# A chunked state-space stage: injection reordered on TensorE and ScalarE, products moved to GpSimd, tables and products of VectorE placed in PSUM

## Chip, cores and metric

The kernel runs on one core of one Trainium2 chip. The metric is device time in microseconds (us), the median of several executions of the whole program. Engines are named as in the profile: PE (TensorE, with PEld for its weight loads), DVE (VectorE), ACT (ScalarE), POOL (GpSimd) and SP (SyncE, which here only issues DMAs).

## What is computed

A two-layer network over 256 tokens of width 2048, in fp32: an S5 state-space mixer with a GLU, a feed-forward layer, shared keys and values with a dilated window attention, and a second feed-forward layer. The change lies in the S5 mixer alone. It has 128 groups of 16 channels, each with 64 complex states:

```python
lb = exp(lam * dt)                              # complex: lb_re, lb_im
bb = (lb - 1) / lam * B                         # input matrix, complex
bu = einsum('blgh,gph->blgp', u, bb)
s[l] = lb * s[l-1] + bu[l]                      # scan over the 256 tokens
y = Re(einsum('blgp,ghp->blgh', s, C)) + d_skip * u
g = gelu(y);  val, gate = split(g @ w_glu);  x = x + val * sigmoid(gate)
```

## The kernel before

The tokens are cut into 64 chunks of four. `s5_glu` does the whole stage; after it, dense blocks of products with weights split into a high and a low part run on PE to the end of the kernel.

The 128 groups are handled in four quarters (`qr` 0 to 3); a half (`h` 0 or 1) is two quarters and has its own state tile `sts[h]`. The parts, in the order in which the code issues them:

- **Tables.** DVE computes `lam` from the inputs, then its second, third and fourth powers (`power`, each kept as a 2x2 real form `pf[k]` by `form`), `gain` (B times a gain, into the last tap of `gps[qr]`), and `coefs` (15 small operations for the factor `cf`). ACT sums squares of the input; POOL raises the mean to -1/2 into `rc`; `scale_x` applies it on ACT.
- **`build_u(h)`**: PE transposes the input, ACT copies it under two masks into `ub[h]`.
- **`taps(qr)`**: for each of three taps and each of two components, a `pair`: one product of 512 columns and one sum of 256 columns on DVE.
- **`taps_inject(qr)`**, four rounds each: four transposes on PE into a `tr` tile, a copy on ACT to `gt`, sixteen products on PE into an `mm` tile, two copies on ACT into `sts`. All rounds stand in this order on PE and on ACT.
- **`build_c`**, **`powers(qr)`**: C times the factor, and C times the four powers (`fds[qr]`), as `pair`s on DVE.
- **`build_m(qr)`**: PE makes the in-chunk matrix of a quarter; `store_m(qr)` adds the skip term `dsm` on DVE and moves shifted rows with six DMAs on SP's queue.
- **`y_local`**: PE products of the in-chunk part.
- **`scan(nm, h)`**: 63 steps for each half, three DVE operations a step (a product of 128 columns with the fourth power's form, two sums of 64); `run` issues the two halves in turn, so six operations make a common step. "Chain a" is half 0, "chain b" half 1.
- **`y_state`** (PE, needs the finished states and `fds`), **`gelu`** (ACT), **`y_T`** (PE transposes, ACT high part, DVE low part), then `products` with the weights that `prepare` loaded and split.

`T`, `A`, `G` and `W` are PE, ACT, POOL and DVE with the order of the code kept: an instruction issued through them never passes an earlier one on its engine.

```python
        T, A, G, W = (InOrder(tc, e) for e in (nc.tensor, nc.scalar, nc.gpsimd, nc.vector))
```

Nearly all of their instructions therefore have line L57 in the profile, that of the wrapper; tiles tell them apart (`act_raw` tiles are called `actr` there). PSUM has eight banks: four for tiles `mm`, two for `tr`, two for `ms`. SBUF pools: `early` is released before the weights are opened, `late` after the mixer, `xres` (tag `xr`) has two buffers.

Of the kernel before, what the change touches and what calls it, by code (L numbers as in the profile page):

```python
# [2 lines left out]

# [8 lines left out]
FP32 = mybir.dt.float32  # L12
# [3 lines left out]
ALU = mybir.AluOpType  # L16
# [3 lines left out]
P = 128  # L20
# [8 lines left out]
GI = 16  # L29
NS = 64  # L30
# [29 lines left out]
class Net:  # L60
# [141 lines left out]
    def s5_glu(self):  # L202
        tc, nc, io = self.tc, self.nc, self.io
        late = tc.alloc_tile_pool(name="s5late", bufs=1)
        early = tc.alloc_tile_pool(name="s5early", bufs=1, side="right")
# [6 lines left out]
        ds = late.tile([P, 2, 64], FP32, name="ds")  # L212
# [30 lines left out]
        def tt(out, i, j, o, eng=None):  # L243
            (eng or V).tensor_tensor(out=out, in0=i, in1=j, op=o)
# [19 lines left out]
        for st in sts:  # L264
            G.memset(st[:, 0], 0.0)
        dsm = late.tile([P, 64, GI], FP32, name="dsm")
        tt(ds[:, 0], ds[:, 0], ds[:, 1], ALU.mult, G)
        tt(dsm, ds[:, 0].unsqueeze(2).broadcast_to([P, 64, GI]),
           dmask.unsqueeze(1).broadcast_to([P, 64, GI]), ALU.mult, G)

        ssc = early.tile([P, 2, 4], FP32, name="ssc")
        for q in range(2):
            for s in range(4):
                junk = early.tile([P, 32, GI], FP32, name="xjunk", tag="gt", bufs=4)
# [64 lines left out]
        gps = [early.tile([P, 2, 16, 4, GI], FP32, name=f"gp{qr}") for qr in range(2)]  # L339
        gps += [self.xres.tile([P, 2, 16, 4, GI], FP32, name="gpx", tag="xr") for _ in range(2)]  # L340

        def gain(qr):
            mo = 16 * qr
# [21 lines left out]
        def pair(out, f, src):  # L365
            pr = early.tile([P, 2, 16, GI], FP32, name="gpr", bufs=2)
            yield lambda: tt(pr, f.unsqueeze(3).broadcast_to([P, 2, 16, GI]), src, ALU.mult, W)
            yield lambda: tt(out, pr[:, 0], pr[:, 1], ALU.add, W)
# [8 lines left out]
        def taps_inject(qr):  # L377
            g, st, mo = gps[qr], sts[qr // 2], 16 * (qr % 2)
            for j2 in range(4):
                gtt = early.tile([P, 2, 2, P], FP32, name="gt", tag="gt", bufs=4)  # L380
                ps = self.ps_tr.tile([P, 2, 2, P], FP32, name="tr")
                for j in range(2):
                    for ri in range(2):
                        T.transpose(out=ps[:, j, ri],
                                    in_=g[:, ri, 4 * j2 + 2 * j:4 * j2 + 2 * j + 2].rearrange("p x s i -> p (x s i)"),
                                    identity=self.ident)
                A.copy(out=gtt, in_=ps)
                ps = self.ps_mm.tile([P, 2, 2, 2, NS], FP32, name="mm")
                for j in range(2):
                    ju = (qr % 2) * 8 + 2 * j2 + j  # L390
                    for ri in range(2):
                        for y in range(2):
                            T.matmul(ps[64 * y:64 * y + 64, j, ri],
                                     lhsT=gtt[:, j, ri, 64 * y:64 * y + 64],
                                     rhs=ub[qr // 2][:, ju, y].rearrange("p x c -> p (x c)"),
                                     start=True, stop=True)
                for j in range(2):
                    m0 = mo + 4 * j2 + 2 * j
                    A.copy(out=st[:, 1:64, :, m0:m0 + 2].rearrange("p c r m -> p r m c"),
                           in_=ps[:, j, :, :, 0:63])  # L400
# [4 lines left out]
        def coefs():  # L405
# [16 lines left out]
            yield lambda: tt(cf[:, 0, 1], t1, den, ALU.mult, W)  # L422
            yield lambda: W.tensor_copy(out=cf[:, 1, 0], in_=cf[:, 0, 1])

        def build_c(qr):
            mo = 16 * qr
            for k in range(2):
                yield from pair(cp[:, k, mo:mo + 16], cf[:, k, :, mo:mo + 16], ct[:, :, mo:mo + 16])

        def m_operand(qr, j4):  # L430
            m0 = 16 * qr + 8 * j4
# [25 lines left out]
                    nc.sync.dma_start(out=mt[64 * xx:64 * xx + n, t, mo:mo + 16],  # L457
                                      in_=mt[64 * xx + 64 - n:64 * xx + 64, 3, mo:mo + 16])

        def scan(nm, h):  # L460
            st = sts[h]
            f = pf[3][:, :, :, 32 * h:32 * h + 32]
            pr = late.tile([P, 2, 2, 32], FP32, name="spr" + nm)
            sm = late.tile([P, 2, 32], FP32, name="ssm" + nm)

            def step(c):
# [5 lines left out]
            for c in range(63):  # L472
                yield from step(c)
# [12 lines left out]

        def powers(qr):
            mo = 16 * qr
            for t in range(4):
                for k in range(2):  # L490
                    yield from pair(fds[qr][:, t, k], pf[t][:, :, k, mo:mo + 16], cp[:, :, mo:mo + 16])

        def y_local(qr, pool, nm):
            pss = [pool.tile([P, 8, 4, GI], FP32, name=nm) for _ in range(2)]
# [62 lines left out]
        fds = {0: fd[:, 0], 1: fd[:, 1]}  # L557
        run(*[build_c(qr) for qr in range(2)])
        run(*[build_c(qr) for qr in range(2, 4)])
        ms = {}  # L560
        for qr in range(4):
            ms[qr] = build_m(qr)
            if qr > 1:
                fds[qr] = self.xres.tile([P, 4, 2, 16, GI], FP32, name="fdx", tag="xr")
            run(powers(qr))
            if qr:
                store_m(qr - 1, ms[qr - 1])
        store_m(3, ms[3])
# [12 lines left out]

        prepare(0)
        y_state(0, yl[0])
        gms = {0: gelu(yl[0])}
        y_state(1, yl[1])
        gtile = [self.act_tile(), None]
        lhs = [gtile[0][:, k] for k in range(8)]
        y_T(0, gms[0])
        gms[1] = gelu(yl[1])
        gb0 = self.open_block(KT)  # L590
        for c in range(4):
            if c + 1 < 4:
                prepare(c + 1)
            for w in ws.pop(c):
                self.products(gb0, w, lhs, T)
            if c < 2:
                yl[c + 2] = y_local(c + 2, self.ps_ms, "ms")
                y_state(c + 2, yl[c + 2])
                gms[c + 2] = gelu(yl[c + 2])
            if c == 1:  # L600
                gtile[1] = self.act_tile()
                lhs += [gtile[1][:, k] for k in range(8)]
            if c < 3:
                y_T(c + 1, gms[c + 1])
# [325 lines left out]
```

## Time and profile before

| | |
|---|---|
| median of 3 runs | 2525.39 us (2515.63 to 2526.24) |
| profiled execution | 2518.62 us, span 2516.4 us |
| PE busy | 2403.2 us (96%) |
| DVE busy | 1361.6 us (54%) |
| ACT busy | 1080.2 us (43%) |
| POOL busy | 41.8 us (2%) |

The span runs from the first to the last instruction. A row of a list of instructions in order of time has its start in us, its length in us, the engine, the line, the operation, the tile written and the tiles read, the count, and in brackets the idle time before it with what ended it. A row that ends in "| a, b | c" is a group: busy time in us, mean length of one in ns, idle time before them in us. "PEclk" is the clock that the throttle granted to PE, 1.00 being full speed.

### The profile page before, as it was taken

Reading aid. Unit: us, or ns where it says so; the run is one execution under the profiler, and the core shown is the slowest. Engines: PE = TensorE matmul, PEld = TensorE weight load, DVE = VectorE, ACT = ScalarE, POOL = GpSimd, SP = SyncE. Lnnn points to the kernel's source line nnn. Section 1 sums busy time; section 2 is a strip of 40 time slices with the busy share of each in tenths; the row PEclk is TensorE's granted clock in tenths of the full one; section 3 lists DMA queues with packets and bytes.
Section 4 is the critical chain, followed back from the end, with each engine's and each line's share of the span. In section 5 each row is a group of like instructions: output and inputs, shape, how many; then the busy total and the mean of one; then the engine's idle time right before and its main releaser. Section 6 shows DMA issues by size and latency. Waiting matters only on the chain.

```text
span 2516.4 us, 28535 instructions
## 1 busy us (share of the span) xinstructions
PE 2403.2 (96%) x11456; PEld 1945.1 (77%) x11456; DVE 1361.6 (54%) x2033; ACT 1080.2 (43%) x1359; POOL 41.8 (2%) x33
## 2 busy tenths in 40 slices
PE   5619999999999999999999999999999999999999
PEld 4508888888888888888888888878888888888887
DVE  9493554544544444455544677765545444444444
ACT  5304444444433444455444555544444443344433
POOL 1000000000000000000000100000000000000000
PEclk7559999999999999999999999999999999999999
DMA  2014555555555555555555444445555555555554
GB/s 81 23 40 134 185 184 184 184 184 184 184 184 186 185 186 181 186 181 193 176 192 184 158 160 151 151 144 174 184 184 184 184 184 186 188 187 179 187 195 148
DMA packets 63028, 423.51 MB, mean 168 GB/s; under 512 B 8112, under 2 KB 9520, under 8 KB 12336
## 3 DMA queue, kind: packets, MB, share of 16 engines
q1 hardware_dynamic: 61744, 419.60, 48.8%
q8 instruction: 89, 1.46, 0.2%
q10 hardware_dynamic: 1152, 2.10, 0.2%
q14 instruction: 43, 0.35, 0.0%
HBM read 418.79 MB, written 2.10 MB: 167 GB/s over the span
## 4 chain that ended last, share of the span: by engine, by line
PE 93%; DVE 3%; ACT 0%; issue 0%; POOL 0%; POOLq 0%
PE mm L120 29%; PE mm L122 29%; PE mm L121 29%; PE ms L57 2%; PE mm L57 1%; PE ms L770 1%; DVE actr L57 1%; PE tr L656 1%; PE tr L721 1%; DVE sprb L57 1%; DVE spra L57 1%; PE tr L770 0%; PE tr L183 0%; DVE gpr L57 0%; DVE ssmb L57 0%; DVE ssma L57 0%
## 5 line engine op out<-in xcount | busy, mean ns | idle before, releaser
L102 DVE TENSOR_TENSOR wlo<-raw,whi 128x1024 fp32r<-128x1024 f32 x776 | 948.8, 1224 | 1002.3 <-ACT whi L101 1000.9
L101 ACT CAST whi<-raw 128x1024 fp32r<-128x1024 f32 x776 | 813.5, 1048 | 1160.4 <-PE mm L122 1143.4
L120 PE MATMUL mm<-whi,actt 128*128 128x512 f32 x3104 | 1235.9, 398 | 1.4 <-ACT whi L101 1.4
L122 PE MATMUL mm<-whi,actt 128*128 128x512 f32 x3104 | 1229.7, 396 | 0.0
L121 PE MATMUL mm<-wlo,actt 128*128 128x512 f32 x3104 | 1229.5, 396 | 0.0
L122 PEld LDWEIGHTS mm<-whi,actt 128*128 128x128 f32 x3104 | 583.2, 188 | 139.4
L120 PEld LDWEIGHTS mm<-whi,actt 128*128 128x128 f32 x3104 | 583.2, 188 | 138.6 <-ACT whi L101 2.1
L121 PEld LDWEIGHTS mm<-wlo,actt 128*128 128x128 f32 x3104 | 583.3, 188 | 137.1 <-DVE wlo L102 0.4
L57 PE MATMUL ms<-actr 128*64 128x64 f32 (+1 forms) x320 | 13.1, 292 | 63.2 <-DVE actr L57 54.2
L57 PEld LDWEIGHTS ms<-actr 128*64 128x64 f32 (+1 forms) x320 | 12.3, 198 | 64.4 <-issue 64.4
L57 ACT ACTIVATE gm<-ms 128x256 f32<-128x256 f32 x12 | 3.6, 390 | 86.3 <-PE ms L57 86.3
L57 PE MATMUL mm<-actr,gt 128*64 128x128 f32 x256 | 25.7, 365 | 14.9 <-ACT gt L57 14.9
L708 POOL TENSOR_TENSOR sc<-ssq,mhalf 128x8 f32<-128x8 f32 x16 | 32.1, 2005 | 474.9 <-DVE ssq L706 474.9
L642 ACT ACTIVATE sg<-mm,r 128x512 f32<-128x512 f32 x44 | 30.1, 689 | 21.3 <-PE mm L122 21.0
L57 PEld LDWEIGHTS mm<-actr,gt 128*64 128x64 f32 x256 | 20.3, 187 | 20.5 <-ACT gt L57 20.5
L779 ACT ACTIVATE s<-s,mx 128x384 f32<-128x384 f32 (+1 forms) x32 | 24.8, 774 | 25.2 <-DVE mx L777 25.2
L646 DVE SCALAR_TENSOR_TENSOR sg<-mm,r,sg 128x512 f32<-128x512 f32 x44 | 30.9, 742 | 0.0
L704 ACT ACTIVATE sq<-mm 128x512 f32<-128x512 f32 x32 | 19.0, 593 | 23.5 <-PE mm L122 23.5
L784 DVE SCALAR_TENSOR_TENSOR p<-s,z,p 128x128 f32<-128x128 f32 (+1 forms) x64 | 26.3, 411 | 3.8 <-ACT p L782 3.6
L57 ACT COPY actr<-mm 128x252 f32<-128x252 f32 x32 | 16.5, 620 | 27.3 <-PE mm L57 27.3
L660 DVE TENSOR_TENSOR actt<-tr,actt 128x512 fp32r<-128x512 f32 x44 | 28.2, 682 | 0.0
L659 ACT CAST actt<-tr 128x512 fp32r<-128x512 f32 x44 | 23.6, 590 | 10.1 <-PE tr L656 10.1
(182 smaller groups left out, 1007.5 us busy)
## 6 DMA issues: line engine op xcount, KB each, us to landing
raw<-w_gu SPq DMA_DIRECT2D x176, 1024.0 KB, 4.9
raw<-w_down SPq DMA_DIRECT2D x88, 1024.0 KB, 4.9
raw<-w_q SPq DMA_DIRECT2D x48, 1024.0 KB, 4.9
raw<-w_glu SPq DMA_DIRECT2D x32, 1024.0 KB, 4.9
raw<-w_kv SPq DMA_DIRECT2D x32, 1024.0 KB, 4.8
raw<-w_o SPq DMA_DIRECT2D x16, 1024.0 KB, 4.8
actr<-x_c SPq DMA_DIRECT2D x2, 1024.0 KB, 6.1
xr<-x_t SPq DMA_DIRECT2D x8, 256.0 KB, 3.7
```

Source lines behind the costliest of these rows:

```text
L57: return lambda *a, **k: self.tc.keep_in_program_order(call(*a, **k))
L101: (scalar or self.nc.scalar).copy(out=hi, in_=r)
L102: (vector or self.nc.vector).tensor_tensor(out=lo, in0=r, in1=hi.bitcast(FP32), op=ALU.subtract)
L120: matmul(ps[th], lhsT=a[:, 0, ts], rhs=hi, start=(k == 0), stop=False)
L121: matmul(ps[th], lhsT=a[:, 0, ts], rhs=lo, start=False, stop=False)
L122: matmul(ps[th], lhsT=a[:, 1, ts], rhs=hi, start=False, stop=(k == n - 1))
L642: nc.scalar.activation(out=s, in_=ps[th], func=AF.Silu, scale=rs[th])
L646: nc.vector.scalar_tensor_tensor(out=sg[th], in0=ps[th], scalar=rs[th], in1=sg[th], op0=ALU.mult, op1=ALU.mult)
L656: nc.tensor.transpose(out=pt[:, k, th * P:(th + 1) * P], in_=sg[th][:, c:c + P], identity=self.ident)
L660: nc.vector.tensor_tensor(out=ht[:, k0:k0 + 2, 1], in0=pt, in1=ht[:, k0:k0 + 2, 0].bitcast(FP32), op=ALU.subtract)
L708: nc.gpsimd.tensor_tensor(out=sc, in0=ssq, in1=self.mhalf.rearrange("p (a b) -> p a b", a=2), op=ALU.pow)
L784: nc.vector.scalar_tensor_tensor(out=pr, in0=sc[:, g], scalar=z, in1=pr, op0=ALU.mult, op1=ALU.add)
```

## The change

- The power tables, gains and coefficients are all computed before the first taps. Three table forms are copied to PSUM (`tabs`).
- `taps` makes four products of 256 columns and two sums per tap, with the tables and half of the products in PSUM; it no longer uses `pair`.
- `taps_inject` is split into `taps_T` and `inject`; the transposes and ACT copy of round i+1 are issued before the products of round i. The products go to `ms` tiles.
- `pair` moves to POOL, and with it `build_c` and `powers`; so does the order of `d_skip`, which now follows `build_c` on POOL.
- The scan keeps the fourth power's form and its products in one PSUM tile and adds both halves of the product to the state in turn. Half 0 runs its first 16 steps alone; `build_m` and `store_m` are issued between common steps; half 1 finishes its last 16 steps while the outputs of half 0 are made.
- The outputs are issued in another order: `y_state` of quarters 0 and 1, their `gelu`, and then each GLU part with its `prepare`.

```diff
...
-        tt(ds[:, 0], ds[:, 0], ds[:, 1], ALU.mult, G)
-        tt(dsm, ds[:, 0].unsqueeze(2).broadcast_to([P, 64, GI]),
-           dmask.unsqueeze(1).broadcast_to([P, 64, GI]), ALU.mult, G)
+        def d_skip():
+            tt(ds[:, 0], ds[:, 0], ds[:, 1], ALU.mult, G)
+            tt(dsm, ds[:, 0].unsqueeze(2).broadcast_to([P, 64, GI]),
+               dmask.unsqueeze(1).broadcast_to([P, 64, GI]), ALU.mult, G)
...
+        gps = [early.tile([P, 2, 16, 4, GI], FP32, name=f"gp{qr}") for qr in range(4)]
+        gpa = [self.ps_mm.tile([P, 16, GI], FP32, name="mm") for _ in range(2)]
+        gpb = [early.tile([P, 16, GI], FP32, name=f"gpb{k}") for k in range(2)]
+        tb2 = self.ps_mm.tile([P, 2, 2, 64], FP32, name="mm")
+        tb = self.ps_mm.tile([P, 2, 2, 2, 64], FP32, name="mm")
+        tabs = [tb[:, 0], tb[:, 1], tb2]
...
             for s in range(2, -1, -1):
+                for r, pr in enumerate((gpa, gpb)):
+                    for k in range(2):
+                        tt(pr[k], tabs[2 - s][:, k, r, mo:mo + 16].unsqueeze(2).broadcast_to([P, 16, GI]),
+                           g[:, r, :, 3], ALU.mult, W)
                 for k in range(2):
-                    yield from pair(g[:, k, :, s], pf[2 - s][:, k, :, mo:mo + 16], g[:, :, :, 3])
+                    tt(g[:, k, :, s], gpa[k], gpb[k], ALU.add, W)
...
+        def pair(out, f, src):
+            pr = late.tile([P, 2, 16, GI], FP32, name="fpr", bufs=2)
+            tt(pr, f.unsqueeze(3).broadcast_to([P, 2, 16, GI]), src, ALU.mult, G)
+            tt(out, pr[:, 0], pr[:, 1], ALU.add, G)
...
-        def scan(nm, h):
+        def scan(h):
             st = sts[h]
+            f, pr = tb[:, 0, h], tb[:, 1, h]
+            f = f.rearrange("p k (r m) -> p k r m", r=2)
+            pr = pr.rearrange("p k (r m) -> p k r m", r=2)
+            for c in range(63):
                 hh, v = st[:, c], st[:, c + 1]
                 yield lambda: tt(pr, f, hh.unsqueeze(1).broadcast_to([P, 2, 2, 32]), ALU.mult, W)
-                yield lambda: tt(sm, pr[:, :, 0], pr[:, :, 1], ALU.add, W)
-                yield lambda: tt(v, v, sm, ALU.add, W)
+                yield lambda: tt(v, v, pr[:, :, 0], ALU.add, W)
+                yield lambda: tt(v, v, pr[:, :, 1], ALU.add, W)
...
+        def steps(n, *its):
+            run(*[itertools.islice(it, 3 * n) for it in its])
...
         power()
         gain(0)
-        power()
         gain(1)
-        for h in range(2):
-            scale_x(h)
-        build_u(0)
-        run(taps(0))
-        taps_inject(0)
         power()
         gain(2)
         gain(3)
-        run(taps(1), coefs())
-        taps_inject(1)
-        build_u(1)
-        run(taps(2))
-        taps_inject(2)
-        run(taps(3))
-        taps_inject(3)
+        power()
+        run(coefs())
+        for k in range(3):
+            W.tensor_copy(out=tabs[k], in_=pf[k])
+        for h in range(2):
+            scale_x(h)
+        for qr in range(4):
+            build_c(qr)
+        d_skip()
+        fds = {qr: self.xres.tile([P, 4, 2, 16, GI], FP32, name="fdx", tag="xr") for qr in range(2)}
+        for qr in range(2):
+            powers(qr)
+        build_u(0)
+        taps(0)
+        gtt = taps_T(0)
+        for i in range(16):
+            if i % 4 == 3 and i < 15:
+                taps(i // 4 + 1)
+            g0, gtt = gtt, taps_T(i + 1) if i < 15 else None
+            inject(i, g0)
+            if i == 6:
+                build_u(1)
         fd = self.act_raw([P, 2, 4, 2, 16, GI])
...
+        for qr in (2, 3):
+            fds[qr] = fd[:, qr - 2]
+            powers(qr)
+        for h in range(2):
+            W.tensor_copy(out=tb[:, 0, h].rearrange("p k (r m) -> p k r m", r=2),
+                          in_=pf[3][:, :, :, 32 * h:32 * h + 32])
+        sa, sb = scan(0), scan(1)
+        steps(LEAD, sa)
+        ms = {qr: build_m(qr) for qr in range(2)}
+        for k, qr in enumerate(range(4)):
+            steps((14, 5, 10, 5)[k], sa, sb)
+            store_m(qr, ms[qr])
+            if qr < 2:
+                ms[qr + 2] = build_m(qr + 2)
...
-        yl = {0: y_local(0, self.ps_ms, "ms"), 1: y_local(1, self.ps_mm, "mm")}
-        run(scan("a", 0), scan("b", 1))
+        yl = {0: y_local(0, self.ps_ms, "ms"), 1: y_local(1, self.ps_tr, "tr")}
+        steps(63 - LEAD - 34, sa, sb)
...
+        steps(4, sb)
         prepare(0)
+        for qr in range(2):
+            y_state(qr, yl[qr])
+        gms = {qr: gelu(yl[qr]) for qr in range(2)}
+        steps(8, sb)
+        channels(0)
         gb0 = self.open_block(KT)
+        for w in ws.pop(0):
+            self.products(gb0, w, lhs, T)
+        yl[2] = y_local(2, self.ps_ms, "ms")
+        run(sb)
+        prepare(1)
+        channels(1)
+        for w in ws.pop(1):
+            self.products(gb0, w, lhs, T)
+        y_state(2, yl[2])
+        gms[2] = gelu(yl[2])
+        yl[3] = y_local(3, self.ps_mm, "mm")
+        y_state(3, yl[3])
+        prepare(2)
+        channels(2)
+        gms[3] = gelu(yl[3])
+        for w in ws.pop(2):
+            self.products(gb0, w, lhs, T)
+        prepare(3)
+        channels(3)
+        for w in ws.pop(3):
+            self.products(gb0, w, lhs, T)
         late.release()
```

`LEAD` is 16. `channels(qr)` is `y_T(qr)` with the allocation of its output tile.

More of the change, by code (lines that the diff above doesn't have):

```diff
@@ L1 @@
+import itertools
 import math
@@ L47 @@
 NW = 14
+LEAD = 16
 class InOrder:
@@ L227, in s5_glu @@
         nc.sync.dma_start(out=self.ident, in_=io["ident"])
-        ct = early.tile([P, 2, 64, GI], FP32, name="ct")
+        ct = self.xres.tile([P, 2, 64, GI], FP32, name="ct", tag="xr")
         nc.sync.dma_start(out=ct, in_=io["c"])
@@ L337, in power @@
             pf.append(form(f"pf{k}", z))
-        gps = [early.tile([P, 2, 16, 4, GI], FP32, name=f"gp{qr}") for qr in range(2)]
-        gps += [self.xres.tile([P, 2, 16, 4, GI], FP32, name="gpx", tag="xr") for _ in range(2)]
+        gps = [early.tile([P, 2, 16, 4, GI], FP32, name=f"gp{qr}") for qr in range(4)]
[4 more added lines that the diff above has]
+        tabs = [tb[:, 0], tb[:, 1], tb2]
         def gain(qr):
@@ L363, in build_u @@
                                  scale=masks[:, xx:xx + 1])
[L365 to L368, printed above, removed]
         def taps(qr):
@@ L373, in taps @@
             for s in range(2, -1, -1):
+                for r, pr in enumerate((gpa, gpb)):
+                    for k in range(2):
+                        tt(pr[k], tabs[2 - s][:, k, r, mo:mo + 16].unsqueeze(2).broadcast_to([P, 16, GI]),
+                           g[:, r, :, 3], ALU.mult, W)
                 for k in range(2):
-                    yield from pair(g[:, k, :, s], pf[2 - s][:, k, :, mo:mo + 16], g[:, :, :, 3])
[L377 to L400, printed above, removed]
@@ new lines, in taps, with taps_T @@
+                    tt(g[:, k, :, s], gpa[k], gpb[k], ALU.add, W)
+        def taps_T(i):
+            g, j2 = gps[i // 4], i % 4
+            gtt = early.tile([P, 2, 2, P], FP32, name="gt", tag="gt", bufs=3)
+            ps = self.ps_tr.tile([P, 2, 2, P], FP32, name="tr")
+            for j in range(2):
+                for ri in range(2):
+                    T.transpose(out=ps[:, j, ri],
+                                in_=g[:, ri, 4 * j2 + 2 * j:4 * j2 + 2 * j + 2].rearrange("p x s i -> p (x s i)"),
+                                identity=self.ident)
+            A.copy(out=gtt, in_=ps)
+            return gtt
@@ new lines, in inject @@
+        def inject(i, gtt):
+            qr, j2 = divmod(i, 4)
+            st, mo = sts[qr // 2], 16 * (qr % 2)
+            ps = self.ps_ms.tile([P, 2, 2, 2, NS], FP32, name="ms")
+            for j in range(2):
+                ju = (qr % 2) * 8 + 2 * j2 + j
+                for ri in range(2):
+                    for y in range(2):
+                        T.matmul(ps[64 * y:64 * y + 64, j, ri],
+                                 lhsT=gtt[:, j, ri, 64 * y:64 * y + 64],
+                                 rhs=ub[qr // 2][:, ju, y].rearrange("p x c -> p (x c)"),
+                                 start=True, stop=True)
+            for j in range(2):
+                m0 = mo + 4 * j2 + 2 * j
+                A.copy(out=st[:, 1:64, :, m0:m0 + 2].rearrange("p c r m -> p r m c"),
+                       in_=ps[:, j, :, :, 0:63])
@@ L427, in build_c @@
             for k in range(2):
-                yield from pair(cp[:, k, mo:mo + 16], cf[:, k, :, mo:mo + 16], ct[:, :, mo:mo + 16])
+                pair(cp[:, k, mo:mo + 16], cf[:, k, :, mo:mo + 16], ct[:, :, mo:mo + 16])
         def m_operand(qr, j4):
@@ L490, in powers @@
                 for k in range(2):
-                    yield from pair(fds[qr][:, t, k], pf[t][:, :, k, mo:mo + 16], cp[:, :, mo:mo + 16])
+                    pair(fds[qr][:, t, k], pf[t][:, :, k, mo:mo + 16], cp[:, :, mo:mo + 16])
         def y_local(qr, pool, nm):
@@ L548, in s5_glu @@
         gain(3)
-        run(taps(1), coefs())
-        taps_inject(1)
-        build_u(1)
-        run(taps(2))
-        taps_inject(2)
-        run(taps(3))
-        taps_inject(3)
-        fd = self.act_raw([P, 2, 4, 2, 16, GI])
[L557 to L568, printed above, removed]
+        power()
[20 more added lines that the diff above has]
+                build_u(1)
+        fd = self.act_raw([P, 2, 4, 2, 16, GI])
+        for qr in (2, 3):
[12 more added lines that the diff above has]
+                ms[qr + 2] = build_m(qr + 2)
         warm = late.tile([P, 1], FP32, name="warm")
@@ L580, in prepare, with channels @@
             ws[c] = [self.split(raw, half, A, W) for half in range(2)]
-        prepare(0)
[L583 to L589, printed above, removed]
-        gb0 = self.open_block(KT)
[L591 to L604, printed above, removed]
+        gtile = {}
+        def channels(qr):
+            if qr % 2 == 0:
+                gtile[qr // 2] = self.act_tile()
+                lhs.extend(gtile[qr // 2][:, k] for k in range(8))
+            y_T(qr, gms[qr])
+        lhs = []
+        steps(4, sb)
+        prepare(0)
+        for qr in range(2):
[3 more added lines that the diff above has]
+        channels(0)
+        gb0 = self.open_block(KT)
+        for w in ws.pop(0):
[19 more added lines that the diff above has]
+            self.products(gb0, w, lhs, T)
         late.release()
```

8 lines of the change are left out of this document (1 added, 7 removed).

## The prediction

> **What bounds the kernel now.** I read the page first (PE 96% busy), then a table of busy times by stage, then the instructions in order of time inside the S5 stage, which is all that the edit touches.
>
> ```profile
> 0.00:18.28 18.28, 6.04 (x32) 5.95 (x32) 14.94 (x75) 8.64 (x21) 6.58 (x11) 1.00 0.76 277
> 18.28:83.86 65.58, 45.20 (x388) 34.45 (x386) 52.82 (x120) 37.74 (x72) 0.00 (x0) 0.71 0.00 1
> 83.86:128.84 44.98, 26.82 (x132) 26.32 (x132) 19.99 (x40) 9.67 (x18) 0.00 (x0) 0.52 0.10 33
> 128.84:188.59 59.75, 5.79 (x125) 5.71 (x125) 59.75 (x379) 0.00 (x0) 0.00 (x0) 0.56 0.12 42
> 188.59:243.22 54.63, 52.48 (x773) 44.68 (x774) 21.22 (x26) 22.80 (x42) 0.00 (x0) 0.94 0.35 117
> 243.22:2516.40 2273.18, 2266.83 (x10013) 1827.95 (x10011) 1192.87 (x1396) 1001.34 (x1209) 35.23 (x22) 1.00 0.53 179
> ```
>
> The columns after the length are busy time (instructions) of PE, PEld, DVE, ACT, POOL, then the clock, DMA share and GB/s. From 243.22 on PE is full, and no edit reaches it: whatever the change wins or loses, it does so before the first dense GLU products. There the bound changes hands: tables (DVE), injection (18.28 to 83.86, a PE/ACT chain), M blocks and power sets (nothing full), scan (DVE alone, 59.75 us), outputs (PE 52.48 of 54.63). POOL does nothing from 18.28 on. The profiled time of 2518.62 us is the span, 2516.40 (last row), plus 2.2.
>
> **The injection** is a round trip: PE waits for ACT's copy, ACT for PE's products.
>
> ```profile
> 26.36 1.98 PE L57 MATMUL mm<-actr,gt 128*64 128x128 f32 x16 [0.68 <-ACT gt L57]
> 28.27 1.12 PE L57 MATMUL tr<-ident,gp 128*128 128x128 f32 x4
> 30.06 1.98 PE L57 MATMUL mm<-actr,gt 128*64 128x128 f32 x16 [0.67 <-ACT gt L57]
> ```
>
> ```profile
> 28.38 1.03 ACT L57 COPY actr<-mm 128x252 f32<-128x252 f32 x2 [2.08 <-PE mm L57]
> 29.42 0.58 ACT L57 COPY gt<-tr 128x512 f32<-128x512 f32 x1
> ```
>
> ```profile
> 47.62 1.09 PE L57 MATMUL mm<-actr,gt 128*64 128x128 f32 x16 [0.98 <-ACT gt L57]
> 48.64 0.65 PE L57 MATMUL tr<-ident,gp 128*128 128x128 f32 x4
> ```
>
> ```profile
> 26.36:44.50 18.14, 15.11 (x100) 0.50 0.00 1
> ```
>
> ```profile
> 52.23 2.46 ACT L57 ACTIVATE actr<-tr,masks 128x512 f32<-128x512 f32 x4
> ```
>
> One of the 16 groups takes 3.70 us at half clock (26.36 to 30.06). The edit issues the next group's transposes ahead of this group's products, so ACT's copy runs under PE. PE's own issue is then 1.91 (26.36 to 28.27) and some 1.04 for the transposes, 2.95 us a group at half clock, and 1.02+0.6 = 1.62 at full clock; ACT's is about 1.04 (28.38 to 29.42) and 0.5. So the two are level at full clock, and PE bounds a group at 1.62 to 2.95 us. The clock stayed at 0.50 for 18 us although PE was busy 15.11 of 18.14, so I take three or four groups cold, then warm, and cold again after the gap at the second `build_u`, whose eight ACT activations (four in 2.46) stand between two groups on ACT's queue and cost 5.3 us in the middle of the chain.
>
> **Tables and taps** (DVE).
>
> ```profile
> 14.68 0.43 DVE L57 TENSOR_TENSOR pr<-pf,lam 128x256 f32<-128x256 f32 x1
> 15.14 0.29 DVE L57 TENSOR_TENSOR pw<-pr 128x128 f32<-128x128 f32 x1
> 15.47 0.40 DVE L57 COPY pf<-pw 128x64 f32<-128x64 f32 x3
> ```
>
> ```profile
> 18.28 0.68 DVE L57 TENSOR_TENSOR gpr<-pf,gp 128x512 f32<-128x512 f32 x1
> 18.99 0.42 DVE L57 TENSOR_TENSOR gp<-gpr 128x256 f32<-128x256 f32 x1
> 19.34 0.68 DVE L57 TENSOR_TENSOR gpr<-pf,gp 128x512 f32<-128x512 f32 x1
> ```
>
> ```profile
> 4.09 1.92 POOL L57 TENSOR_TENSOR dsm<-ds,dmask 128x1024 f32<-128x1024 f32 x1
> 4.10 1.97 DVE L236 TENSOR_SCALAR e1n<-e1t 128x64 f32<-128x64 f32 x1
> ```
>
> Two spacings follow: an operation that needs the one before starts 0.03 to 0.04 us after its end (15.14+0.29, then 15.47); one that doesn't starts earlier, a 256-wide one 0.35 after its predecessor (18.99 to 19.34). Moved ahead of the first taps: the third power (1.2: 14.68 and on through its four 64-wide forms), two gains of 512 (0.6 each, as the 512-wide product without its wait), the 15 coefficient operations of 64 (an estimate of 2.6, by the two spacings, with a reciprocal of 0.5) and three 256-wide table copies (1.0): +6.0. Against it: `d_skip` leaves the start, where DVE's 64-wide operation was held for 1.97 us, precisely while POOL multiplied. DVE gets that back until the `rc` operation needs PE's sums: -1.1. Taps start at 18.28+6.0-1.1 = 23.2. A set is 18 operations of 256 instead of 6 pairs at 1.06: 18x0.335 = 6.05 against 6.4, no difference worth counting. The sets end at 29.3, 35.3, 41.4 and 47.4; PE's first group starts at 29.3.
>
> Chain a needs groups 0 to 7: 29.3 + 1.1 + three cold groups 8.9 + four warm 6.6 + 5.3 + one group and its copy 2.8 = **54** (48.5 all warm, 60 all cold). Chain b needs the other eight: 54 + 15.8 = **70** (62.5 to 84).
>
> **Power sets and C products** leave DVE.
>
> ```profile
> L57 DVE TENSOR_TENSOR gpr<-pf,cp 128x512 f32<-128x512 f32 x32 | 21.9, 684 | 0.1
> ```
>
> ```profile
> L57 POOL TENSOR_TENSOR ds<-ds 128x64 f32<-128x64 f32 x1 | 0.3, 314 | 0.0
> ```
>
> ```profile
> L708 POOL TENSOR_TENSOR sc<-ssq,mhalf 128x8 f32<-128x8 f32 x16 | 32.1, 2005 | 474.9 <-DVE ssq L706 474.9
> ```
>
> ```profile
> 83.86 12.45 PE L57 MATMUL ms<-cb,gp 128*128 128x64 f32 x64 [1.79 <-ACT cb L57]
> ```
>
> ```profile
> 111.04 0.88 DVE L57 TENSOR_TENSOR actr<-ms,dsm 64x256 f32<-64x256 f32 x2
> ```
>
> ```profile
> 128.09 6.60 SPq L457 DMA_DIRECT2D actr<-actr  x9
> ```
>
> The row's 32 pairs and eight for C, at 1.06 each (18.28 to 19.34), are 42.4 us of DVE that go. POOL's price isn't shown for 512 columns. Its products of 64 and 1024 columns (0.314, 1.92) give 1.68 ns a column: 1.06 + 0.64 = 1.70 us a pair. POOL's queue, in order: C products from 22.2, `d_skip` 2.2, then four power sets of eight pairs: C at 36, sets at 52, 65, 79, 93. Who waits: the M blocks for C (70), `store_m` for `d_skip` (84), the output products for the sets (118 and later). The slack is 25 us or more, so I cost it at nothing. From below nothing, since POOL was idle; from above the row of the power function, 2.0 us for 8 columns, taken as a fixed cost (a rival below). The M blocks (12.45 for two) go to PE under the scan: ready at 79, 85, 91 and 98, wanted by DVE at 84, 89, 100 and 105. If chain b starts at 84, both move with it. `store_m`'s 24 DMAs now go out on SP's queue between scan steps; the last six leave at 106 and, at 0.73 us each (6.60 for nine), are out by 111, ahead of the `y_local` products that chain a's end covers. The first weight load, queued behind them, is wanted at 122. Nothing for either; without that cover, their 4.4 us.
>
> **Scan.**
>
> ```profile
> 130.80 0.28 DVE L57 TENSOR_TENSOR spra<-pf,actr 128x128 f32<-128x128 f32 x1
> 131.00 0.28 DVE L57 TENSOR_TENSOR sprb<-pf,actr 128x128 f32<-128x128 f32 x1
> 131.21 0.21 DVE L57 TENSOR_TENSOR ssma<-spra 128x64 f32<-128x64 f32 x1
> ...
> 131.75 0.28 DVE L57 TENSOR_TENSOR spra<-pf,actr 128x128 f32<-128x128 f32 x1
> ```
>
> ```profile
> 1569.23 0.68 DVE L773 SCALAR_TENSOR_TENSOR s<-dm,tr 128x128 f32<-128x128 f32 x3 [1.48 <-PE tr L770]
> ```
>
> Both chains interleaved take 0.945 us a step (130.80 to 131.75) in six operations, as after the edit. One chain alone is all dependent: 0.28+0.21+0.21 and three gaps of 0.035 = 0.82. So the 16 lead steps cost 13.1, 54 to 67, inside the wait for chain b's groups (70). Then 47 common steps (44.4) and four `store_m` (3.6). What no row shows is DVE writing PSUM, nor a read behind it. Reading PSUM costs nothing extra: three 128-wide operations in 0.68 are 0.20 apart, like 130.80 and 131.00. Lower bound: 0.945 a step. Upper bound: every operation waits for the last, both chains 2x0.82 = 1.63. I take 0.945, nearest the reading row. Chain a ends at 70.5+44.4+3.6 = **118.5** (110 to 130; with the upper step 151), now 188.5.
>
> The Trainium skill, "Perfetto Trace Analysis", section "Optimizing Scalar/DVE Operations", puts DVE's overhead per instruction at about 60 ns on SBUF and 125 on PSUM. The reading row disagrees with it (0.20 both ways); for writes no run here shows it. Taken at its word, 65 ns on each of some 330 operations would be 21 us and a time near 2474.
>
> **Outputs.**
>
> ```profile
> 188.59 4.95 PE L57 MATMUL ms<-actr 64*64 64x64 f32 x128 [53.85 <-DVE actr L57]
> ...
> 199.38 0.61 DVE L57 TENSOR_TENSOR actt<-tr,actt 128x256 fp32r<-128x256 f32 x1 [8.54 <-ACT actt L57]
> ...
> 242.83 0.40 PE L57 MATMUL mm<-whi,actt 128*128 128x512 f32 x1
> ```
>
> PE's work behind chain a is the same: 188.6 to 242.8, less some 1.0 us of the next block's products in between: 53.3. Chain b's last 16 steps (13.1) run beside it. Twelve of them and a weight split (2.4) stand on DVE ahead of its first low-part copy: 12.2 after the chain, against 10.9 now (199.38): +1.3; four more and a split ahead of the second: +0.9. So 55.5.
>
> **Sum:** 118.5+55.5 = 174 against 188.6+53.3 = 241.9: -67.9, and 2518.62-67.9 = 2450.7. The median of the three runs is 6.8 above the profiled one, and one run is 3 below it, so I add 2: **2453**.
>
> **The rivals.**
> (1) *PSUM products cost the scan.* A product written to the bank that holds the other chain's table and product makes the next operation wait, as in a single chain: steps of 1.15 to 1.63 instead of 0.945, 47 times: +10 to +32, so 2463 to 2485. For: no row shows such a write. Against: the reading row.
> (2) *DVE and POOL lock each other out.* The 4.10 row is such a hold. If it also meets operations with a PSUM operand, DVE stands still for POOL's 40x1.70 = 68 us: 2519 to 2523. Against: in the new order DVE has one SBUF input in each operation from the table copies on, and the held one had SBUF alone. The Trainium skill, "Perfetto Trace Analysis", in the section named, says that offloading between DVE and GpSimd might not help, since they share an SBUF port; the Trainium skill, "SBUF — State Buffer", section "SBUF: two separate sides", limits that lock to DVE's 2-port modes and to two SBUF inputs. The held row agrees with both; no run here shows a PSUM operand beside POOL.
> (3) *POOL is too slow: slower than before.* If an instruction has the power row's 2.0 us as a fixed cost, a pair is 5.3 us, the last set ends at 24.4+212 = 236, and the last output products (4.95) and two GLU parts (an estimate of 7.5 each) end at 256 instead of 241.9: 2533. It decides from 4.9 us a pair on (24.4+40x4.9+20 = 240). Against: 64 columns in 0.314.
> (4) *The pipeline does not speed PE up*: all cold, +12, 2463: inside the forecast's own range.
>
> **How the numbers follow.** Forecast 0.62 (own range 2440 to 2466), rival 1 0.18, rival 2 0.12 (a quarter of it a partial hold near 2490), rival 3 0.04, better than 2440 0.04. The range 2438 to 2492 holds 0.83. Within 0.5% (about 12 us, the spread of the three runs) lie most of rival 2 and nothing else; so faster 0.87, same 0.08, slower 0.05.
>
> **What would show it.** PE group spacing 1.6 to 3.0 us in the injection; taps from 23 to 47 without a break; POOL pairs near 1.7 us, ending near 93, with no DVE operation stretched beside them; DVE's first scan step at 54 and common steps 0.945 apart from 70; chain a's end near 118 and the dense products from 174. Wrong it would be if common steps are over 1.2, if DVE idles for `store_m`, or if DVE durations grow while POOL runs.

## The result, and the profile after

The changed kernel takes 2459.39 us (median, 2457.45 to 2460.36), against 2525.25 us for the kernel before beside it: ratio 0.9747, 95% interval 0.9722 to 0.9771. The forecast was 2453 us, with a range of 2438 to 2492. The profiled execution took 2457.45 us with a span of 2455.6, so 60.8 us of span are gone where the sum had 67.9.

The table by stage of the changed kernel, columns as before (length, then busy time of PE, PEld, DVE, ACT and POOL, the clock, DMA share, GB/s):

```profile
0.00:23.77 23.77, 9.13 (x64) 8.79 (x64) 19.12 (x101) 14.99 (x32) 5.32 (x11) 0.97 0.59 213
23.77:48.33 24.56, 16.94 (x190) 13.97 (x192) 24.42 (x76) 16.72 (x33) 23.54 (x27) 0.78 0.01 2
48.33:63.63 15.30, 15.12 (x166) 11.71 (x162) 11.86 (x48) 12.45 (x26) 14.67 (x18) 0.84 0.01 2
63.63:128.70 65.07, 32.27 (x256) 31.53 (x257) 60.07 (x290) 11.30 (x22) 32.65 (x38) 0.58 0.17 61
128.70:183.00 54.30, 51.87 (x770) 43.95 (x771) 32.34 (x74) 21.59 (x40) 0.00 (x0) 0.94 0.35 118
183.00:2455.60 2272.60, 2266.21 (x10016) 1824.99 (x10014) 1193.31 (x1397) 1002.54 (x1210) 35.29 (x22) 1.00 0.52 180
```

The last row is 2272.60 us long; before it was 2273.18. So the whole gain lies ahead of the dense products, as the prediction had it. The stages are new: tables, taps (DVE 24.42 of 24.56 busy), chain a's lead (15.30), both chains together (65.07, DVE 60.07), outputs.

The injection, as PE's instructions in order of time (start, length; the wrapper's line is L59 here), and PE's clock in one stretch of it (the number ahead of the DMA share):

```profile
33.67 1.09 PE L59 MATMUL ms<-actr,gt 128*64 128x128 f32 x16
...
35.28 1.09 PE L59 MATMUL ms<-actr,gt 128*64 128x128 f32 x16
...
47.38 1.97 PE L59 MATMUL ms<-actr,gt 128*64 128x128 f32 x16 [1.65 <-ACT actr L59]
...
33.67:42.75 9.08, 9.08 (x117) 7.21 (x116) 9.08 (x29) 8.49 (x18) 8.69 (x10) 1.00 0.00 0
```

A group takes 1.61 us (33.67 to 35.28) instead of 3.70. Between the groups PE now waits for ACT only once, 1.65 us behind the second `build_u`. Its clock is 1.00 from the second group on, but the two groups behind that wait are slow again (1.97 us at 47.38, 1.98 at 50.33).

DVE at the start, at the taps, and at the first steps of chain a:

```profile
3.98 0.20 DVE L238 TENSOR_SCALAR e1n<-e1t 128x64 f32<-128x64 f32 x1
...
23.77 0.76 DVE L59 TENSOR_TENSOR mm<-mm,gp 128x256 f32<-128x256 f32 x2
...
48.33 0.30 DVE L59 TENSOR_TENSOR mm<-mm,actr 128x128 f32<-128x128 f32 x1
50.45 0.47 DVE L59 TENSOR_TENSOR actr<-actr,mm 128x64 f32<-128x64 f32 x2 [1.83 <-ACT actr L59]
50.96 0.30 DVE L59 TENSOR_TENSOR mm<-mm,actr 128x128 f32<-128x128 f32 x1
...
51.81 0.30 DVE L59 TENSOR_TENSOR mm<-mm,actr 128x128 f32<-128x128 f32 x1
...
63.63 0.70 DVE L59 TENSOR_TENSOR mm<-mm,actr 128x128 f32<-128x128 f32 x2
```

The operation that was held for 1.97 us takes 0.20 without POOL's product beside it. The taps start at 23.77, the input of chain a is there at 50.45, a step of a single chain takes 0.85 us (50.96 to 51.81), and the first common step stands at 63.63. From 23.77 to chain a's end DVE waits for another engine only once, the 1.83 us ahead of the first sum.

Common steps, again DVE in order of time, while POOL is done with everything:

```profile
100.83 0.63 DVE L59 TENSOR_TENSOR mm<-mm,actr 128x128 f32<-128x128 f32 x2
101.50 0.62 DVE L59 TENSOR_TENSOR actr<-actr,mm 128x64 f32<-128x64 f32 x4
102.15 0.63 DVE L59 TENSOR_TENSOR mm<-mm,actr 128x128 f32<-128x128 f32 x2
```

One step takes 1.32 us between these rows (100.83 to 102.15; 1.314 over a longer stretch), not 0.945. Two products of 0.30 take 0.63 together, so the second starts 0.03 after the end of the first, and the first sum 0.04 after the end of the second (100.83+0.63 = 101.46, then 101.50). These are the gaps of operations that need the one before. Before, two products started 0.20 apart.

POOL: its group of set products, and a pair in order of time; then PE at the end of chain a and at the last product of the first GLU block:

```profile
L59 POOL TENSOR_TENSOR fpr<-pf,cp 128x512 f32<-128x512 f32 x32 | 33.9, 1059 | 0.0
...
39.46 1.06 POOL L59 TENSOR_TENSOR fpr<-pf,cp 128x512 f32<-128x512 f32 x1
40.60 0.73 POOL L59 TENSOR_TENSOR fdx<-fpr 128x256 f32<-128x256 f32 x1
41.29 1.06 POOL L59 TENSOR_TENSOR fpr<-pf,cp 128x512 f32<-128x512 f32 x1
...
128.70 4.82 PE L59 MATMUL ms<-fdx,actr 64*64 64x64 f32 x126 [11.88 <-DVE actr L59]
...
183.39 0.39 PE L59 MATMUL mm<-whi,actt 128*128 128x512 f32 x1
```

A pair on POOL takes 1.83 us (39.46 to 41.29). Chain a ends at 128.70 instead of 188.59, and the outputs behind it take 54.69 (before 242.83-188.59 = 54.24).

### The profile page after: what moved, and what is told of

Read it like the earlier page. It is cut to its first block, busy times and chain, and to the rows that moved or that the text cites. A ratio compares the mean times of both kernels' runs of the same rounds, so it can differ in the third digit from the quotient of the medians.

```text
span 2455.6 us, 28577 instructions
## 1 busy us (share of the span) xinstructions
PE 2391.6 (97%) x11456; PEld 1934.9 (79%) x11456; DVE 1341.1 (55%) x1982; ACT 1079.6 (44%) x1359; POOL 111.5 (5%) x113
## 4 chain that ended last, share of the span: by engine, by line
PE 94%; DVE 4%; ACT 1%; issue 0%; DMA 0%; POOL 0%; SPq 0%; DVEq 0%; POOLq 0%
PE mm L123 29%; PE mm L122 29%; PE mm L124 29%; DVE actr L59 2%; DVE mm L59 2%; PE mm L59 1%; PE ms L811 1%; PE tr L697 1%; PE ms L59 1%; PE tr L762 1%; PE tr L811 0%; PE tr L185 0%; PE ms L841 0%; PE tr L59 0%; DMA actr<-x_c 0%
## 5 line engine op out<-in xcount | busy, mean ns | idle before, releaser
L59 DVE TENSOR_TENSOR actr<-actr,mm 128x64 f32<-128x64 f32 x252 | 43.1, 217 | 5.6 <-ACT actr L59 1.8
L59 DVE TENSOR_TENSOR mm<-mm,actr 128x128 f32<-128x128 f32 x126 | 37.7, 299 | 4.4
L683 ACT ACTIVATE sg<-mm,r 128x512 f32<-128x512 f32 x44 | 30.1, 688 | 21.3 <-PE mm L124 21.0
L59 POOL TENSOR_TENSOR fpr<-pf,cp 128x512 f32<-128x512 f32 x32 | 33.9, 1059 | 0.0
L59 PE MATMUL ms<-cb,gp 128*128 128x64 f32 x128 | 26.7, 407 | 7.3 <-DVE actr L59 5.5
L59 PEld LDWEIGHTS ms<-cb,gp 128*128 128x128 f32 x128 | 26.2, 317 | 7.9 <-issue 5.9
```

The lines of the kernel that those rows point to most:

```text
L59: return lambda *a, **k: self.tc.keep_in_program_order(call(*a, **k))
L683: nc.scalar.activation(out=s, in_=ps[th], func=AF.Silu, scale=rs[th])
```

## The experiments

Theory A says that the injection, POOL and the chip's reads and writes of PSUM behave as forecast, and that the common step is longer because the kernel's instructions wait for each other: both chains share one PSUM tile, and an access to a PSUM tile waits for the last access to any part of it where one of the two writes. In the program's list both products and the first sum of a common step wait on the instruction right ahead on DVE; before, each wait was at least one instruction further back. The rivals: the chip itself is slow with products in PSUM, DVE is held by POOL, or the gain is not from the parts that were thought to bring it.

**1. A PSUM tile for each chain.**

```diff
-            f, pr = tb[:, 0, h], tb[:, 1, h]
+            f, pr = sct[h][:, 0], sct[h][:, 1]
...
+        sct = [self.ps_mm.tile([P, 2, 2, 2, 32], FP32, name="mm") for _ in range(2)]
```

> Each chain has its form and its product in a PSUM tile of its own, in two banks; all else as in the changed kernel. Theory A: the common step went from 0.945 to 1.314 us because, with both chains in one PSUM tile, the program makes each product and each first sum wait for the instruction right before it on DVE. Then the step falls to 0.95 to 1.0 us, chain a ends near 112 instead of 128.7, and the time falls by 15 to 17 us, to about 2443. Theory B: DVE's writes to PSUM are slow in themselves. Then the step stays at 1.25 us or more and the time within 3 us of 2459.

Measured: 2441.86 us (2440.51 to 2443.98), ratio to the kernel before 0.9705 (0.9677 to 0.9732). DVE's common steps, and PE at the end of chain a:

```profile
108.83 0.49 DVE L59 TENSOR_TENSOR mm<-mm,actr 128x128 f32<-128x128 f32 x2
109.23 0.61 DVE L59 TENSOR_TENSOR actr<-actr,mm 128x64 f32<-128x64 f32 x4
109.76 0.49 DVE L59 TENSOR_TENSOR mm<-mm,actr 128x128 f32<-128x128 f32 x2
...
111.71 4.94 PE L59 MATMUL ms<-fdx,actr 64*64 64x64 f32 x128 [6.12 <-DVE actr L59]
```

The step is 0.93 us, table and product still in PSUM, and chain a ends 17.0 us earlier (128.70 to 111.71). This version beats both kernels: by 17.5 us the changed one.

**2. Two tiles cut the other way.** Both tables in one tile, both products in the other; beside it the changed kernel once more on the same chip.

```diff
-            f, pr = sct[h][:, 0], sct[h][:, 1]
+            f, pr = sct[0][:, h], sct[1][:, h]
```

> The kernel with two scan tiles, but cut the other way: both chains' tables in one PSUM tile, both chains' products in the other, so that a table is no longer in the bank into which products are written, while the chains share a tile of products again. Theory A (the kernel's own ordering: an access to a tile waits for the last write to any part of it, and for its last reads before a write; in the program's list both products and the first sum of a common step wait on the instruction right ahead): the step is that of the changed kernel, 1.31 us, chain a's end near 129, the time 2459 within 4 us. Rival B (the chip is slow when an operation writes a product into the bank from which the next one reads a table): the step falls to between 0.92 and 1.1, the time to 2442 to 2449.

> The changed kernel as it is, on the same chip as the kernel with shared products, so that the two are compared beside each other: 2459 within 3 us, common step 1.314 us. Theory A has both equal within 3 us; rival B has this one 10 us or more longer.

Measured: 2459.78 us (2458.13 to 2460.18), the changed kernel beside it 2459.69 (2457.48 to 2460.47). DVE's common steps with shared products:

```profile
100.80 0.63 DVE L59 TENSOR_TENSOR mm<-mm,actr 128x128 f32<-128x128 f32 x2
...
102.12 0.63 DVE L59 TENSOR_TENSOR mm<-mm,actr 128x128 f32<-128x128 f32 x2
```

The step is back at 1.32 us, with the tables in another bank than the products. So it isn't the writing of a product beside a table: experiment 1 has that too, and is fast. What the slow versions have in common is that both chains' products share a PSUM tile. Whether the chip alone, without the waits, would be slow when both chains' products lie in one bank was not tried.

**3. The scan in SBUF**: the form from `pf[3]`, the product in the free coefficient tile, a half for each chain.

```diff
-            f, pr = tb[:, 0, h], tb[:, 1, h]
+            f = pf[3][:, :, :, 32 * h:32 * h + 32]
+            pr = cf[:, h].rearrange("p k (r m) -> p k r m", r=2)
```

> The scan's form and product lie in SBUF, as in the kernel before, so that its operations have two SBUF inputs; the product takes the place of the factor tile, whose last reader is long done. All else as in the changed kernel, POOL's products too. Theory A (POOL and DVE lock each other out when a DVE operation has two SBUF inputs): steps of the lead and common steps beside POOL, until POOL ends, take 1.5 us or more, POOL's pairs grow beyond 2 us, steps after POOL's end take 0.945, and the time is 2465 or more. Theory B (no such lock; only operations with one SBUF input and none in PSUM are held): all common steps 0.945, the time near 2443.

Measured: 2474.46 us (2474.16 to 2475.77), ratio 0.9832 (0.9809 to 0.9855). DVE and POOL while both run, then DVE after POOL's end:

```profile
52.28 1.05 DVE L59 TENSOR_TENSOR cform<-pf,actr 128x128 f32<-128x128 f32 x1
53.36 1.73 DVE L59 TENSOR_TENSOR actr<-actr,cform 128x64 f32<-128x64 f32 x2
55.12 0.84 DVE L59 TENSOR_TENSOR cform<-pf,actr 128x128 f32<-128x128 f32 x1
...
52.12 1.06 POOL L59 TENSOR_TENSOR fpr<-pf,cp 128x512 f32<-128x512 f32 x1
53.26 0.73 POOL L59 TENSOR_TENSOR fdx<-fpr 128x256 f32<-128x256 f32 x1
53.95 1.06 POOL L59 TENSOR_TENSOR fpr<-pf,cp 128x512 f32<-128x512 f32 x1
...
104.56 0.50 DVE L59 TENSOR_TENSOR cform<-pf,actr 128x128 f32<-128x128 f32 x2
...
105.51 0.50 DVE L59 TENSOR_TENSOR cform<-pf,actr 128x128 f32<-128x128 f32 x2
```

With both inputs in SBUF a single chain's step takes 2.84 us beside POOL (52.28 to 55.12) instead of 0.85, and DVE's operations end just behind POOL's instructions (52.28+1.05 = 53.33, POOL 53.18). With POOL done the step is 0.95. So the PSUM inputs are what keeps DVE going beside POOL: the hold that rival 2 feared exists, but did not meet operations with a PSUM input. The 0.95 also narrows Theory A: here both products are halves of one SBUF tile (`cform`), and neither the step nor the program's list shows a wait for the neighbour. It is the sharing of a PSUM tile that costs. POOL's pair stays at 1.83: the expectation that its pairs would grow was wrong, DVE alone paid here.

**4. The pairs back on DVE.**

```diff
-            tt(pr, f.unsqueeze(3).broadcast_to([P, 2, 16, GI]), src, ALU.mult, G)
-            tt(out, pr[:, 0], pr[:, 1], ALU.add, G)
+            tt(pr, f.unsqueeze(3).broadcast_to([P, 2, 16, GI]), src, ALU.mult, W)
+            tt(out, pr[:, 0], pr[:, 1], ALU.add, W)
```

> The C products and power sets go back to DVE, at their place in the new order; all else as in the changed kernel. Theory A: DVE is the bound from the tables to the end of chain a, so all 40 pairs at 1.06 us show: +42, to about 2501, and POOL's move was worth two thirds of the whole gain. Rival: most of them find room while DVE waits for PE's injection, and the time is 2459 to 2475.

Measured: 2500.21 us (2499.9 to 2502.15), ratio 0.9935 (0.9912 to 0.9958), 41 us over the changed kernel. The work that went to POOL, as a group of DVE, and PE at chain a's end:

```profile
L59 DVE TENSOR_TENSOR fpr<-pf,cp 128x512 f32<-128x512 f32 x32 | 22.0, 686 | 0.0
...
171.37 4.91 PE L59 MATMUL ms<-fdx,actr 64*64 64x64 f32 x127 [10.53 <-DVE actr L59]
```

Chain a ends 42.7 us later (171.37 against 128.70), which is the 42.4 us of pairs that the prediction took from DVE. The move to POOL is the largest part of the gain, and a full one.

**5. No overlap in the injection**: a round's transposes are issued after the products of the round before.

```diff
-            g0, gtt = gtt, taps_T(i + 1) if i < 15 else None
-            inject(i, g0)
+            inject(i, gtt)
+            gtt = taps_T(i + 1) if i < 15 else None
```

> The transposes of an injection round are issued behind the products of the round before, as in the kernel before; all else as in the changed kernel. Theory A: a round takes 2.65 us at full clock instead of 1.61, chain a starts 8 us later and chain b 17 later, and since DVE then has nothing else to do, the time grows by 15 to 30 us (more if PE's clock stays low): 2475 to 2490. Rival: the lead steps hide it, and the time is within 5 us of 2459.

Measured: 2479.65 us (2474.55 to 2489.12), ratio 0.9856 (0.9825 to 0.9888), 20 us over the changed kernel. PE in order of time, the clock in the first stretch, and chain a's first sum and end:

```profile
31.20 1.97 PE L59 MATMUL ms<-actr,gt 128*64 128x128 f32 x16 [0.68 <-ACT gt L59]
...
67.73 1.09 PE L59 MATMUL ms<-actr,gt 128*64 128x128 f32 x16 [0.97 <-ACT gt L59]
...
31.20:55.51 24.31, 20.04 (x137) 15.32 (x137) 17.05 (x53) 9.74 (x18) 23.29 (x27) 0.50 0.01 2
...
64.41 0.48 DVE L59 TENSOR_TENSOR actr<-actr,mm 128x64 f32<-128x64 f32 x2 [16.02 <-ACT actr L59]
...
149.99 4.75 PE L59 MATMUL ms<-fdx,actr 64*64 64x64 f32 x126 [11.70 <-DVE actr L59]
```

The waits of 0.68 us are back, and the clock is 0.50 for the whole stretch, although PE is busy 20.04 of 24.31 us. Without breaks (9.08 of 9.08) it was 1.00. All eight groups of chain a run at the low clock. But the waits alone don't set it: from 65.09 on the same run has full clock (1.09 us for the products) with waits of 0.97 us. What brings the clock up there is not shown. DVE waits 16.02 us for chain a's input, and chain a ends 21.3 us later (149.99 against 128.70), which covers the 20 us whole.

**6. No lead**, on the version with two tiles: `LEAD = 0` instead of 16.

> The kernel of the experiment with two scan tiles (2441.86 us, chain a's end at 111.7), with a lead of 0 steps instead of 16: both chains start together, so chain a too waits for the last injection group (62.35). Theory A (DVE's queue sets the end of chain a, and the lead fills a wait of DVE for the second half of the injection): DVE idles from 48 to 62; 63 common steps of 0.924 are 58.2, with four stores of 3.6 chain a ends at 63.5+58.2+3.6 = 125 instead of 111.7; chain b's tail beside the outputs is gone, worth up to 2.2: +11 to +13, so 2453 to 2455. Rival B (a lead only moves DVE time from one chain to the other, and the outputs behind chain a wait for chain b later): 2442 within 3 us, with the outputs shorter by what chain a's end is later.

Measured: 2455.85 us (2455.18 to 2457.83), ratio 0.9755 (0.9722 to 0.9788), 14 us over the version with two tiles. DVE's wait, and chain a's end:

```profile
64.15 0.48 DVE L59 TENSOR_TENSOR actr<-actr,mm 128x64 f32<-128x64 f32 x3 [12.70 <-ACT actr L59]
...
126.14 4.91 PE L59 MATMUL ms<-fdx,actr 64*64 64x64 f32 x128 [21.57 <-DVE actr L59]
```

The wait for the second half of the injection is what the lead fills; the 14.4 us of chain a's end (126.14 against 111.71) come out in the time whole. Without a lead chain b ends with chain a, and the outputs are no shorter for it, so chain b's later end costs them nothing. Theory A had allowed up to 2.2 us for that, and its 2453 to 2455 came out just short.

**7 and 8. How much slack POOL has**, on the version with two tiles: each product of a pair issued twice, then three times.

> The kernel with two scan tiles, every product of GpSimd's 40 pairs issued twice: a pair takes 1.82+1.06 = 2.88 us. C is then done at 22.3+8x2.88 = 45.3 and the sets at 70.5, 93.6, 116.6 and 139.7; the third set is wanted at 139.4 and the fourth at 146.3, the C products at 63.5. Theory A (GpSimd has the slack that the prediction named, and DVE's operations with a PSUM operand do not wait for it): 2442 within 3 us, DVE's common step 0.924 unchanged although GpSimd now runs beside all of it. Rival B (GpSimd is near the path): +10 us or more. Rival C (DVE is slowed beside GpSimd after all, in steps that now lie beside it and did not before, 98 to 112): common steps there longer than 0.95.

> The same with every product of GpSimd's pairs issued three times: a pair takes 3.93 us; C is done at 53.7, the sets at 87.4, 118.9, 150.3 and 181.7, wanted at 111.7, 116.4, 139.4 and 146.3. Theory A (the slack ends near 3.0 us a pair): the fourth set is late by 181.7-146.3 = 35 us, so about 2477, and PE waits for GpSimd in the outputs. Rival B (the sets are hidden whatever they take): 2442. Rival C (DVE too is held by the longer GpSimd work): 2490 or more, with chain a's end later than 111.7.

Measured: twice 2444.06 us (2443.6 to 2445.24), thrice 2489.84 (2488.27 to 2490.18); ratios 0.9706 (0.9668 to 0.9745) and 0.9887 (0.9854 to 0.9921). DVE's weight split in the version with two tiles, then that split and POOL with products twice, then PE with products thrice:

```profile
115.00 2.35 DVE L59 TENSOR_TENSOR wlo<-raw,whi 128x1024 fp32r<-128x1024 f32 x2
```

```profile
114.88 3.63 DVE L59 TENSOR_TENSOR wlo<-raw,whi 128x1024 fp32r<-128x1024 f32 x2
...
115.80 1.62 POOL L59 TENSOR_TENSOR actr<-fpr 128x256 f32<-128x256 f32 x1
```

```profile
112.09 4.88 PE L59 MATMUL ms<-fdx,actr 64*64 64x64 f32 x128 [6.99 <-DVE actr L59]
...
190.18 0.57 PE L59 MATMUL mm<-actr 64*64 64x64 f32 x8 [23.87 <-POOL actr L59]
```

Twice the products cost 2.2 us, within the 3 expected: they put POOL beside DVE's weight splits (`wlo<-raw,whi`), which have both inputs in SBUF, and there each holds the other (two split operations 3.63 instead of 2.35, a POOL sum 1.62 instead of 0.73). Three times the products make PE wait for the sets, of which the wait for the fourth, 23.87, is the longest. The time is 48 us longer rather than the 35 expected: a pair took 4.08 us and not 3.93, and more beside the splits. That is about the time that rival C named, but its sign is missing: chain a's end hardly moved (111.71, 112.09). So POOL has slack up to some 3 us a pair and the changed kernel uses 1.83; rival 3 was right in kind, and far off.

**9. Tables and C products behind the first taps**, with a lead of 13, on the version with two tiles.

```diff
         power()
         gain(0)
-        gain(1)
         power()
-        gain(2)
-        gain(3)
         power()
-        run(coefs())
...
         taps(0)
         gtt = taps_T(0)
+        for qr in range(1, 4):
+            gain(qr)
+        run(coefs())
+        for qr in range(4):
+            build_c(qr)
+        d_skip()
+        for qr in range(2):
+            powers(qr)
```

> The kernel with two scan tiles, with the coefficient operations, three of the four gains and all of GpSimd's pairs moved behind the first set of taps, and a lead of 13 steps: PE's first injection group starts some 4 us earlier (25 instead of 29.6), and DVE loses its break of 2 us ahead of chain a's first sum. Theory A (DVE's queue is full from the tables to chain a's end, so only its breaks can be won): chain a's end at 109.5 to 110, time 2439 to 2441, 1 to 3 us less. Rival B (PE's injection sets chain a's end): 4 us less, 2438. Rival C (C comes too late for the M blocks, or gains run beside GpSimd and are held): no gain or a loss of some us.

Measured: 2441.3 us (2441.18 to 2442.51), ratio 0.9697 (0.9668 to 0.9725): no difference from the version with two tiles that these runs can tell. PE and DVE in order of time:

```profile
24.79 1.99 PE L59 MATMUL tr<-ident,gp 128*128 128x128 f32 x8 [3.54 <-DVE gp L59]
...
35.42 0.79 PE L59 MATMUL tr<-ident,gp 128*128 128x128 f32 x4 [2.76 <-DVE gp L59]
...
59.43 2.15 PE L59 MATMUL ms<-actr,gt 128*64 128x128 f32 x32
...
62.67 0.48 DVE L59 TENSOR_TENSOR actr<-actr,mm 128x64 f32<-128x64 f32 x3 [2.27 <-ACT actr L59]
...
112.63 4.86 PE L59 MATMUL ms<-fdx,actr 64*64 64x64 f32 x128 [9.16 <-DVE actr L59]
```

PE starts 4.8 us earlier (29.62 before that), and waits 2.76 us for the second set of taps. Its last two groups start at 59.43 instead of 61.27, so 1.8 us of the head start are left. With a lead of only 13 steps DVE still waits 2.27 us for chain b's input, and chain a ends 0.9 us later (112.63 against 111.71). Theory A and rival B expected a gain that did not come. Rival C's "no gain" came, but not for its reason: the gains are over (26.8) before POOL starts (29.5), and the M blocks start earlier (63.38 instead of 65.23). The head start was given back in part at the next set of taps, and the shorter lead took the rest. A lead of 16 with this order was not tried.

## Why the prediction was right, and where a step was off

The time was 6.4 us above the forecast and inside its own range. By the steps of the sum, in the profiled execution:

- **Start of the taps**: 23.2 forecast, 23.77 measured, with the held operation back at 0.20 us.
- **Sets of taps**: 6.05 each forecast; forecast to end at 47.4; the last ends shortly ahead of chain a's first product at 48.33, and DVE is busy 24.42 of the 24.56 us between. Right.
- **Injection**: chain a's input at 54 forecast, 50.45 measured. The mis-sized term is the clock: the first three groups were taken as cold, and PE was at full clock from the second one on. The cold group behind the second `build_u` came as forecast. Chain b's input moved with it, to about 64 (64.15 in experiment 6, where DVE waits for it), near its warm bound of 62.5: common steps from 70.5 forecast, from 63.63 measured: -6.9. Rival 4, all groups cold, did not come; experiment 5, without the overlap, has that for chain a's eight groups.
- **Lead**: the prediction's parts of a single chain's step add up to 0.805 us, not to its 0.82, and 0.85 was measured; on 16 steps that is half a microsecond.
- **POOL**: 1.70 us a pair forecast, 1.83 measured (a 512-wide product 1.06 as taken, a sum 0.73 instead of 0.64); the last set at 97.8 instead of 93, still ahead of chain a's end. The cost of nothing was right, and experiments 7 and 8 show how far it reaches.
- **Rival 2** (0.12): refuted for this kernel. Common steps take 1.31 to 1.32 us beside POOL (65 to 97) and behind it (100.83 to 102.15) alike. Experiment 3 shows the hold where both inputs are in SBUF. The Trainium skill, "SBUF — State Buffer", section "SBUF: two separate sides", has the lock only for 2-port modes and two SBUF inputs, and gives it to whoever comes first for its whole instruction; the traces agree on the two inputs, and experiment 7 shows it holding either side. The operation of the 4.10 row has one SBUF input; whether it ran in a 2-port mode no row shows.
- **Common step**: the step that failed. Forecast 0.945 "nearest the reading row", measured 1.314: 47 x 0.369 = +17.3 us on the sum; the four stores took some 3.3 instead of 3.6, which leaves the stage at 65.07 against 48.0. This is rival 1 (0.18) in its place and its size: it gave steps of 1.15 to 1.63, +10 to +32. Its mechanism was only half right. A product in the tile that holds the other chain's does make the next operation wait, but by a wait that the program has, and not by a price of writing PSUM: with a tile for each chain the step is 0.93, below the 0.945 of SBUF. (A price of the shared bank by itself was not separated.) That both chains' products are slices of one PSUM tile stands in the change; that the program waits on this shows in its list of instructions.
- The Trainium skill, "Perfetto Trace Analysis", section "Optimizing Scalar/DVE Operations", with its 125 ns against 60, gives an estimate of 0.945+6x0.065 = 1.335 us for the step, near the 1.314 that came, and 2474 for the time, farther off than the forecast. Experiment 1 does not bear it out: there all six operations of a step read PSUM and two write it, in 0.93 us, which leaves no room for 65 ns more in each.
- **Chain a's end**: 118.5 forecast, 128.70 measured: -6.9 and +17.1 make the +10.2.
- **Outputs**: +2.2 against before forecast, +0.45 measured (54.69 against 54.24): -1.8. Chain b's tail costs them nothing, as experiment 6 shows too.

So it was in part luck that the forecast's own range held: one term, the common step, was 17 us short, and half of that was covered by a clock that came up sooner (-6.9) and by cheaper outputs (-1.8). The way of the gain, and the parts that bring it, were forecast for the right reasons (experiments 4 to 6). Without the shared tile the same sum would have been some 11 us too long: the version with two tiles is at 2441.86.

## What to carry to other kernels

Two independent chains that are interleaved to hide each other's latency need PSUM tiles of their own: slices of one PSUM tile brought back the wait for the neighbour, 0.39 us on a step of 0.92 us, while halves of one SBUF tile did not (experiment 3). Work moved to POOL was free here while each of DVE's operations beside it had an operand in PSUM; with both inputs in SBUF (experiment 3), and in the operation from SBUF to SBUF of the 4.10 row, DVE was held. So put the tables and products that DVE reads in that time into PSUM, and look for long SBUF operations, like weight splits, that POOL's end would slide into. Taking out PE's short waits was worth more here than the waits themselves: six of chain a's eight groups ran at full clock, and none in experiment 5.

## What the runs showed of the hardware

- PE's clock: 0.50 over 24.31 us in which PE was busy 82% with waits of 0.68 to 0.73 us (experiment 5), 1.00 over 9.08 us in which it was busy throughout (changed kernel, up in the second group after the start at 29.62), and full clock too with waits of 0.97 us (experiment 5, from 65.09 on). What decides between them is open.
- DVE with two SBUF inputs beside POOL: short operations (0.28 and 0.21 us) last until POOL's instruction ends, a step 2.84 instead of 0.85, while POOL loses next to nothing (1.07 us a product against 1.06). Beside 1.2 us splits POOL loses too: a sum 1.62 instead of 0.73.
- Writing a 128-wide product to PSUM takes 0.29 to 0.30 us instead of 0.28 in SBUF, with the same 0.20 us between two that don't need each other (experiment 1: two in 0.49 us).
